# The memory norm's weights moved into the memory's weight tiles, with a TensorE warm-up on zeros (two-layer encoder, one core)

## The chip, the cores and the metric

The kernel runs on one core of a Trainium2 chip. A core has a matrix engine (TensorE, PE in the profile; its weight loads are shown apart as PEld), a vector engine (VectorE, DVE), an activation engine (ScalarE, ACT), a general one (GpSimd, POOL) and a sequencer that only issues transfers (SyncE, SP). Each engine works through its own instructions in order and waits on semaphores for the others. The metric is the device time of one execution in microseconds (us), less is better.

## The reference

Two layers over 512 tokens of 1024 features. In each layer the tokens and the 256 rows of a memory are normalised, the normalised memory is projected to keys and values, tokens attend to it, and the result joins another mixer's. What matters here is the memory's part:

```
def rmsnorm(x, g):
    xf = x.astype(jnp.float32)
    y = xf * lax.rsqrt(jnp.mean(xf * xf, axis=-1, keepdims=True) + EPS)
    return (y * g.astype(jnp.float32)).astype(x.dtype)
...
    kv = jnp.einsum('bnd,de->bne', mem_h, w_kv).reshape(Bn, N, 2, MEM_HEADS, HEAD_DIM)
    k = rmsnorm(kv[:, :, 0], kn_g)
    v = kv[:, :, 1]
...
    for i in range(DEPTH):
        h = rmsnorm(x, norm_g[i])
        mem_h = rmsnorm(mem, mem_norm_g[i])
...
        o_mem = memory_attention(q_mem, mem_h, w_mem_kv[i], mem_qn_g[i], mem_kn_g[i])
```

`mem` and its rows' factors are the same in both layers; only the norm's weights `mem_norm_g[i]` (1024 per layer) differ.

## The kernel before

**Products.** Matmuls run in a 32-bit format of fewer mantissa bits (`F32R`). Each factor is split into a high part, rounded, and a low part, the rest: a product is high x high and high x low (`mm_early`, L176 and L177) and, once the weights' low part is there, low x high (`mm_late`, L180). Weights come from `wall`, tiles of 128 x 1024 (512 KB), in the order of `PLAN`/`SEQ`. For each tile `W.hi` casts the high part on ACT (L323, `wl` to `wh`) and `W.lo` subtracts on DVE (L333, `wo`); `wh` and `wo` have four buffers each (`RING`). The first eight tiles, kind "T2", are the memory's key and value weights of layer 0; eight of kind "T2b" are those of layer 1. Two tiles feed the two pieces of a group of eight early and four late matmuls.

**Activations.** A block of tokens or memory is normalised (squares on ACT, L523, or L1132 for the memory; the sum, `mse`, and the power, `rstd`, on POOL, L483 and L484; the multiply by factor and row of weights on DVE, `norm_2`, L530), transposed in 128 x 128 pieces on PE against an identity (`turn4`, L536), and split by `split` (high on ACT, L164, or on DVE, L166; low on DVE, L167) into `act` tiles for the memory, or kept as f32 for x.

**The head** (from L1048). The identity comes by a DMA of ACT's queue (L1054). SP's queue first brings `row0`, the 1024 memory weights of layer 0 as one row (4 KB, L1056), then halves and tiles of the memory `m`, weight tiles two by two, x's row of weights and four tiles of x. `spread` (L1118) multiplies a column of ones by `row0`, so that PSUM holds the weights on all partitions; `times` (L1128) multiplies the memory by them on DVE; `turn4` and `split` make the `act` blocks, named (b, j): rows b*128 and up, features j*512 and up. The rows' factors aren't applied there: `square` and `factor` (L1132 to L1140) put them into `rm`, by which `ev_k` scales the squares of the keys (`head_sq`, L629) and the keys' factor (L694), and `ev_v` the values (L707). `ahead` is called from inside the first projection, and makes (1, 0) and the next weight tiles in the first group, and (0, 1), (1, 1) in the second.

**Layer 1.** `mem_norm(1)` loads the memory again and layer 1's weights as a row on all partitions (`row_load`), multiplies by `rm` and the row (`norm_2`, four DVE operations), transposes and splits; `ev_k` and `ev_v` then need no factor.

**Order.** The instructions of each engine stand in the order in which the code is run: the head is written out, and after it a `Driver` calls generators slot by slot. Nothing reorders them later; a transfer of SP waits for the eighth before it.

Of the kernel before, what the change touches and what calls it, by code (L numbers as in the profile page):

```python
# [10 lines left out]
F32 = mybir.dt.float32  # L11
F32R = mybir.dt.float32r
AF = mybir.ActivationFunctionType
ALU = mybir.AluOpType
# [12 lines left out]
MEM_D = 4  # L27
PAUSE = 2
DIRECT, DIRECT_B = (7,), (3, 4, 5, 6, 7)
LO_K, TURN_K, HI_V, LO_V = (4, 4), (8, 6), (1, 6), (9, 2)  # L30
PD = 2
EO = 2, 2, 1, 2, 2, 1
YB = {"m": (2, 2), "k": (1, 1, 1), 0: (1, 2, 1), 1: (1, 2, 1)}
Y = [3, 2, 2, 2, 3, 2, 2, 1, 1, 1]
# [3 lines left out]
PLAN = ["W2"] + ["T2"] * 2 + ["W1", "W2s"] + ["W2" if c.isdigit() else "W1" for c in A_ORDER[1:]] + ["W2"] + ["O1"] * 2 + ["T2b"] * 2 + ["W1bs", "W2c"] + ["W1b"] * 4 + ["W2b", "W1o"]  # L38
# [93 lines left out]
def trunk_kernel(ctx: ExitStack, tc: tile.TileContext, x, mem, wall, norm_g, mem_norm_g, gcol,  # L132
                 qn_a, kn_a, qn_b, kn_b, ident_d, mask_d, tab_a, tab_b, out):
    nc = tc.nc
# [21 lines left out]
    def at(name="at"):  # L156
        return psum.tile([128, 512], F32, tag="at", name=name, bufs=4)
# [4 lines left out]
    def split(hi, lo, src, act=True):  # L162
        if act:
            A.copy(hi, src)  # L164
        else:
            V.tensor_copy(hi, src)  # L166
        V.tensor_tensor(lo, src, hi.bitcast(F32), ALU.subtract)  # L167
# [28 lines left out]
    class Weights:  # L196
# [80 lines left out]
        def sum(self, force=False, want=None):  # L277
# [33 lines left out]
                return True  # L311
            return False

        def hi(self, force=False):
            i = self.n_hi
            if i >= len(self.items) or not self.ripe(self.at, self.items[i], force, 1 if self.items[i][1] == "T1" and self.items[i][0] < T1_DMA else None):
                return False
            if i >= RING and self.last[i - RING] > self.g - (not force and self.items[i - RING][1] != "P"):
                return False
            self.n_hi += 1  # L320
            wh = pool.tile([128, 1024], F32R, tag="wh", name="wh", bufs=RING)
            wo = pool.tile([128, 1024], F32R, tag="wo", name="wo", bufs=RING)
            A.copy(wh, self.tile[self.items[i]])  # L323
            self.hi_at.append(self.g)
            self.op.append((wh, wo))
            return True

        def lo(self):
            i = self.n_lo
            self.n_lo += 1  # L330
            wh, wo = self.op[i]
            key = self.items[i]
            V.tensor_tensor(wo, self.tile[key], wh.bitcast(F32), ALU.subtract)  # L333
            self.lo_at[key] = self.g
            self.use(key)

# [150 lines left out]

    ident = pool.tile([128, 128], F32, name="ident")
    gc = pool.tile([128, 10], F32, name="gc")
    gk = pool.tile([128, 3], F32, name="gk")  # L490
    tabs = pool.tile([128, 2048], F32, tag="tabs", name="tabs", bufs=1)
    mask = tabs[:, 0:512]
    ropeA = tabs[:, 512:2048].rearrange("p (c b s e) -> p c b s e", c=2, b=4, s=6)
    half = pool.tile([128, 8], F32, name="half")
    rm = pool.tile([128, 6], F32, name="rm")
    ones = tabs[0:1, 0:128]
    V.memset(half, -0.5)
    V.memset(ones, 1.0)
    A.activation(small.tile([128, 1], F32, tag="sm1", name="warm"), half[:, 0:1], AF.Exp)

    class Act:
# [26 lines left out]
    def norm_2(xb, r, row, js=(0, 1)):  # L528
        for j in js:
            V.scalar_tensor_tensor(xb[j], xb[j], r, row[j], ALU.mult, ALU.mult)  # L530

    def turn4(src, hi, lo, mid=None):

        p = at("xT")
        for k in range(4):
            T.transpose(p[:, k * 128:(k + 1) * 128], src[:, k * 128:(k + 1) * 128], ident)  # L536
        p = p.rearrange("p (k t) -> p k t", k=4)
        if mid:
            mid()
        if hi is not None:  # L540
            split(hi, lo, p)
        return p
# [82 lines left out]
    def head_sq(p, n=4, by=QS):  # L625
        ss = sm(n, "hss")
        for j in range(n):
            jk = small.tile([128, 128], F32, tag="junk", name="junk", bufs=2)
            A.activation(jk, p[:, j * 128:(j + 1) * 128], AF.Square, scale=by, accum_out=ss[:, j:j + 1])  # L629
        return rstd_of(ss, n)  # L630
# [20 lines left out]
    def row_load(name, src):  # L651

        t = m4(name="row")
        nc.sync.dma_start(t, src.to_broadcast([128, D]))
        rows[name] = halves(t)
# [1 line left out]
    Ms = {}  # L657

    def mem_norm(layer):
        row_load("m", mem_norm_g[layer:layer + 1, :])  # L660
        t = [m4(name="m") for _ in range(2)]
        for b in range(2):
            nc.sync.dma_start(t[b], mem[b * 128:(b + 1) * 128])
        t = [halves(v) for v in t]
        yield MEM_D
        norm_2(t[0], rm[:, 0:1], rows["m"])
        yield 1
        norm_2(t[1], rm[:, 1:2], rows["m"])
        M = Act(NM)
        for b in range(2):  # L670
            for j in range(2):
                norm_3(t[b], M, b * 128, j)
            yield 1
        Ms[layer] = M
# [9 lines left out]
    def mem_kv(layer, M, mid=None):  # L684
        kt_ = [m4(F32R, "kmT").rearrange("p (h t) -> p h t", h=4) for _ in range(2)]
        vt_ = [m4(F32R, "vm").rearrange("p (b e) -> p b e", b=2) for _ in range(2)]
        raw = None if layer else m4(name="vr")

        def ev_k(b, p):
            r = head_sq(p) if layer else head_sq(p, by=rm[:, 2 + b:3 + b])  # L690

            def rest():
                if not layer:
                    G.tensor_scalar(r, r, rm[:, b:b + 1], None, ALU.mult)  # L694
                xn = head_mul(p, r)
                yield TURN_K[layer]
                q = transpose4(xn)
                cs = slice(b * 128, (b + 1) * 128)
                yield from put_norm(q, gk_m[layer], kt_[0][:, :, cs], kt_[1][:, :, cs], LO_K[layer])

            drv.release(rest(), 2)
            yield 1

        def ev_v(b, p):

            t = s2(name="vr") if layer else raw[:, b * 512:b * 512 + 512]
            A.activation(t, p, AF.Copy, scale=0.5 if layer else rm[:, 4 + b:5 + b])  # L707
            yield HI_V[layer]
            A.copy(vt_[0][:, b], t)
            yield LO_V[layer]  # L710
            V.tensor_tensor(vt_[1][:, b], t, vt_[0][:, b].bitcast(F32), ALU.subtract)
            yield 1

        proj_t(M, NAT[:2], ev_k, mid)
        proj_t(M, NAT[:2], ev_v)
        return kt_, vt_

# [333 lines left out]
    xt = [m4(name="x") for _ in range(4)]  # L1051
    rows = {}
    mt = [m4(name="m") for _ in range(2)]
    nc.scalar.dma_start(ident, ident_d)  # L1054
    row0 = m4(name="row0")[0:1, :]
    nc.sync.dma_start(row0, mem_norm_g[0:1, :])  # L1056
    nc.sync.dma_start(mt[0][:, 0:512], mem[0:128, 0:512])
    W.dma(2)
    nc.sync.dma_start(mt[1], mem[128:256])
# [49 lines left out]
                            grA[:, None].to_broadcast([128, 4, 6, 32]), ALU.mult)  # L1109
            yield 1  # L1110

    row = [at("row") for _ in range(2)]

    def spread(j, *cols):

        for c in cols:
            cs = slice(256 * c, 256 * c + 256)
            T.matmul(row[j][:, cs], ones, row0[:, 512 * j + 256 * c:512 * j + 256 * c + 256], start=True, stop=True, skip_group_check=True)  # L1118

    spread(0, 0, 1)  # L1120
    mb, M = [halves(t) for t in mt], Act(NM)
    ss = [sm(2, "ss") for _ in range(2)]
    mg = {}

    def times(b, j):

        t = mg[b, j] = s2(name="mg")
        V.tensor_tensor(t, mb[b][j], row[j], ALU.mult)  # L1128

    def square(b, j):  # L1130

        A.activation(s2(name="sq"), mb[b][j], AF.Square, scale=1.0 / 32.0, accum_out=ss[b][:, j:j + 1])  # L1132

    def factor(b):

        e = sm(1, "mse")
        G.tensor_tensor(e, ss[b][:, 0:1], ss[b][:, 1:2], ALU.add)
        r = rstd_of(e, 1)
        for k, by in enumerate((1.0, QS, 0.5)):
            G.tensor_scalar(rm[:, 2 * k + b:2 * k + b + 1], r, by, None, ALU.mult)  # L1140

    def place_m(b, j, act=True, p=None):

        cs = slice(b * 128, (b + 1) * 128)
        split(M.block(0, j, cs), M.block(1, j, cs), p or turn4(mg[b, j], None, None), act)

    square(0, 0)
    times(0, 0)
    spread(1, 0)
    p = turn4(mg[0, 0], None, None)  # L1150
    spread(1, 1)
    W.hi(True)
    place_m(0, 0, False, p)
    W.hi(True)
    W.lo()
    times(1, 0)
    W.lo()
    for b, j in ((1, 0), (0, 1), (1, 1)):
        square(b, j)
    for b in range(2):  # L1160
        times(b, 1)
        factor(b)

    def ahead(u, b):

        if (u, b) == (0, 0):
            place_m(1, 0)
            W.hi(True)
            W.hi(True)
        if (u, b) == (0, 1):  # L1170
            place_m(0, 1)
            place_m(1, 1)

    drv.spawn(prep(), PD)
    drv.spawn(setup(), SET_AT)
# [611 lines left out]
```

## Time and profile before

| | us |
|---|---|
| three runs | 942.2, 943.04 (median), 943.81 |
| the profiled execution's own time | 942.24 |
| its span in the profile | 940.5 |
| DVE busy | 798.6 |
| ACT busy | 691.3 |
| POOL busy | 346.0 |

The span runs from the first instruction in the profile to the last; the time has about 2 us around it. A row of the timeline has the start, the duration, the engine, the line of the code, the operation, output and input, the shapes and types, and in brackets how long the engine had been idle and what ended that. Rows with "x2" and more join neighbours, and their duration reaches from the first's start to the last's end. Operations on one engine overlap a little at their ends, so that the distance of two starts says more than a duration. A row of the windows has, for each engine, busy time and in brackets the number of operations, and at its end PE's granted clock, the DMA engines' share and GB/s.

### The profile page before, as it was taken

The numbers are of one execution on the slowest core, as the hardware profiler recorded it, in microseconds if no ns is written. First come the engines' busy times: TensorE is split into PE (matmuls) and PEld (weight loads), VectorE is DVE, ScalarE is ACT, GpSimd is POOL, SyncE is SP. The second block draws the span as 40 slices with busy tenths as digits, with TensorE's granted clock in tenths as the row PEclk, the third lists the DMA queues.
The fourth block names the chain that finished last, engine by engine and source line by source line (L and its number), as shares of the span: only waits on it lengthen the run. The fifth ranks groups of instructions, "written<-read, shape, count | busy, mean of one in ns | idle before, by whom it ended". The sixth has DMA issues, their size and how long they took to land.

```text
span 940.5 us, 16300 instructions
## 1 busy us (share of the span) xinstructions
PE 932.8 (99%) x5500; PEld 819.9 (87%) x5500; DVE 798.6 (85%) x1442; ACT 691.3 (74%) x1720; POOL 346.0 (37%) x494
## 2 busy tenths in 40 slices
PE   8999999999999999999999999999999999999998
PEld 6889888888888888888889998888988999999886
DVE  6898676879888888889788899977998998689977
ACT  7775788677768686867675667637878887789774
POOL 3411425455554545463836111114262440111123
PEclk9999999999999999999999999999999999999999
DMA  9999937869787878696867889979985686785777
GB/s 355 386 259 336 299 91 190 278 139 256 158 250 147 260 154 268 158 268 136 249 165 206 246 200 243 305 229 326 270 203 122 166 239 168 199 221 126 190 173 179
DMA packets 89429, 207.15 MB, mean 220 GB/s; under 512 B 25217, under 2 KB 34689, under 8 KB 89346
## 3 DMA queue, kind: packets, MB, share of 16 engines
q1 hardware_dynamic: 68818, 140.64, 43.4%
q0 software_dynamic: 19520, 63.97, 36.9%
q10 hardware_dynamic: 1008, 1.51, 0.4%
q8 instruction: 43, 0.70, 0.3%
q14 instruction: 40, 0.33, 0.1%
HBM read 158.31 MB, written 11.08 MB: 180 GB/s over the span
## 4 chain that ended last, share of the span: by engine, by line
PE 91%; DVE 4%; DMA 3%; ACT 1%; issue 0%; SPq 0%; DVEq 0%; ACTq 0%
PE pj L176 24%; PE pj L177 24%; PE pj L180 23%; PE qT L641 2%; DMA og<-od 2%; PE ptb L1616 1%; PE sa L1302 1%; PE oo L1410 1%; PE pt L1389 1%; DMA wl<-in_wall_dram 1%; PE xT L536 1%; PE sa L1298 1%; DVE wo L333 1%; PE ob L180 1%; PE ob L177 1%; PE ob L176 1%
## 5 line engine op out<-in xcount | busy, mean ns | idle before, releaser
L333 DVE TENSOR_TENSOR wo<-wl,wh 128x1024 fp32r<-128x1024 f32 x258 | 316.4, 1232 | 7.0 <-ACT wh L323 6.8
L323 ACT CAST wh<-wl 128x1024 fp32r<-128x1024 f32 x258 | 271.7, 1060 | 29.7 <-PE pj L177 15.6
L176 PE MATMUL pj<-wh,hS 128*128 128x512 f32 (+1 forms) x416 | 154.3, 380 | 0.0
L177 PE MATMUL pj<-wh,hS 128*128 128x512 f32 (+1 forms) x416 | 148.9, 367 | 0.0
L176 PE MATMUL pj<-wh,h 128*128 128x512 f32 (+1 forms) x312 | 115.2, 378 | 0.0
L177 PE MATMUL pj<-wh,h 128*128 128x512 f32 (+1 forms) x312 | 111.7, 367 | 0.0
L484 POOL TENSOR_TENSOR rstd<-mse,half 128x4 f32<-128x4 f32 (+2 forms) x98 | 103.0, 1051 | 8.2
L180 PE MATMUL pj<-wo,hS 128*128 128x512 f32 (+1 forms) x416 | 99.5, 366 | 0.0
L177 PEld LDWEIGHTS pj<-wh,hS 128*128 128x128 f32 x416 | 78.7, 189 | 11.3
L176 PEld LDWEIGHTS pj<-wh,hS 128*128 128x128 f32 x416 | 78.6, 189 | 11.1 <-DVE sn L420 0.2
L483 POOL TENSOR_SCALAR mse<-hss 128x4 f32<-128x4 f32 (+1 forms) x88 | 46.1, 524 | 103.2 <-ACT junk L629 95.5
L180 PEld LDWEIGHTS pj<-wo,hS 128*128 128x128 f32 x416 | 72.4, 189 | 13.1
L629 ACT ACTIVATE junk<-sn 128x128 f32<-128x128 f32 x264 | 79.3, 311 | 2.2 <-DVE sn L411 2.1
L1246 POOL TENSOR_TENSOR ta<-sn,tabs 128x128 f32<-128x128 f32 (+1 forms) x64 | 35.9, 567 | 120.1 <-DVE sn L634 92.8
L398 ACT COPY sn<-pj 128x512 f32<-128x512 f32 x122 | 67.2, 590 | 16.6 <-PE pj L180 15.8
L180 PE MATMUL pj<-wo,h 128*128 128x512 f32 (+1 forms) x312 | 74.5, 365 | 0.0
L307 POOL DMA_DIRECT2D wl<-wl x34 | 30.2, 898 | 114.8 <-DVE wo L333 74.6
L261 POOL DMA_DIRECT2D wl<-in_wall_dram x40 | 38.1, 968 | 81.6 <-DMA wl<-in_wall_dram 35.3
L420 DVE TENSOR_TENSOR sn<-pj,sn 128x512 f32<-128x512 f32 x89 | 60.8, 684 | 7.1 <-PE pj L180 6.6
L177 PEld LDWEIGHTS pj<-wh,h 128*128 128x128 f32 x312 | 59.0, 189 | 8.4
L176 PEld LDWEIGHTS pj<-wh,h 128*128 128x128 f32 x312 | 59.0, 189 | 8.2
L180 PEld LDWEIGHTS pj<-wo,h 128*128 128x128 f32 x312 | 54.3, 189 | 9.7
(283 smaller groups left out, 2366.7 us busy)
## 6 DMA issues: line engine op xcount, KB each, us to landing
wl<-in_wall_dram SPq DMA_DIRECT2D x224, 512.0 KB, 7.5
wl<-wl POOLq DMA_DIRECT2D x68, 512.0 KB, 5.5
wl<-in_wall_dram POOLq DMA_DIRECT2D x44, 512.0 KB, 8.3
od<-o SPq DMA_DIRECT2D x11, 256.0 KB, 5.1
og<-od SPq DMA_DIRECT2D x10, 256.0 KB, 9.8
x<-in_x_dram SPq DMA_DIRECT2D x4, 512.0 KB, 9.0
v0d<-sn SPq DMA_DIRECT2D x8, 256.0 KB, 10.5
acc<-in_x_dram POOLq DMA_DIRECT2D x8, 256.0 KB, 7.1
```

What stands on the lines that cost most here:

```text
L176: T.matmul(o, a, b, start=start, stop=False, skip_group_check=True)
L177: T.matmul(o, c, d, start=False, stop=False, skip_group_check=True)
L180: T.matmul(o, a, b, start=False, stop=stop, skip_group_check=True)
L261: queue.dma_start(t, wall[d], **how)
L323: A.copy(wh, self.tile[self.items[i]])
L333: V.tensor_tensor(wo, self.tile[key], wh.bitcast(F32), ALU.subtract)
L398: A.copy(t, b)
L420: V.tensor_tensor(t, b, t, ALU.subtract if q == "12" else ALU.add)
L483: G.tensor_scalar(e, ss, EPS, None, ALU.add)
L484: G.tensor_tensor(r, e, half[:, 0:n], ALU.pow)
L629: A.activation(jk, p[:, j * 128:(j + 1) * 128], AF.Square, scale=by, accum_out=ss[:, j:j + 1])
L1246: G.tensor_tensor(ta[:, 0:n], xn[:, 0:n, 0:32], ropeA[:, 0, b, s0:s0 + n], ALU.mult)
```

## The change

The memory is transposed raw in both layers. Since (m * g) W is m (g W), the norm's weights go to the weight tiles: they are loaded as 16 rows of 128 (`gm`, both layers), transposed by PE and copied to `gmc`, where column 8 * layer + k holds the weights of features 128 k to 128 k + 127 on the partitions. Of each "T2" and "T2b" tile `hi` makes two ACT activations with a column of `gmc` as scale, and `lo` two DVE multiply-and-subtract operations. `row0`, `spread`, `times` and layer 1's row with its `norm_2` go. Layer 1's keys and values take the rows' factors as layer 0's do. The identity is made on POOL from a cleared tile. PE multiplies zeros six times ahead of the first transpose and five times behind the first memory block's. The squares and factors move behind the last memory blocks.

```diff
+WARM = 6, 5
...
+        def gains(self, key):
+
+            if PLAN[key[0]] not in ("T2", "T2b"):
+                return None
+            n = 8 * (PLAN[key[0]] == "T2b") + 2 * key[2]
+            return [(slice(512 * h, 512 * h + 512), gmc[:, n + h:n + h + 1]) for h in range(2)]
...
-            A.copy(wh, self.tile[self.items[i]])
+            key = self.items[i]
+            if self.gains(key):
+                for c, g in self.gains(key):
+                    A.activation(wh[:, c], self.tile[key][:, c], AF.Copy, scale=g)
+            else:
+                A.copy(wh, self.tile[key])
...
-            V.tensor_tensor(wo, self.tile[key], wh.bitcast(F32), ALU.subtract)
+            if self.gains(key):
+                for c, g in self.gains(key):
+                    V.scalar_tensor_tensor(wo[:, c], self.tile[key][:, c], g, wh[:, c].bitcast(F32), ALU.mult, ALU.subtract)
+            else:
+                V.tensor_tensor(wo, self.tile[key], wh.bitcast(F32), ALU.subtract)
...
-    ones = tabs[0:1, 0:128]
+    zero = tabs[:, 0:128]
+    G.memset(zero, 0.0)
     V.memset(half, -0.5)
-    V.memset(ones, 1.0)
...
-        row_load("m", mem_norm_g[layer:layer + 1, :])
...
-        yield MEM_D
-        norm_2(t[0], rm[:, 0:1], rows["m"])
-        yield 1
-        norm_2(t[1], rm[:, 1:2], rows["m"])
+        yield MEM_D + 1
...
-            r = head_sq(p) if layer else head_sq(p, by=rm[:, 2 + b:3 + b])
+            r = head_sq(p, by=rm[:, 2 + b:3 + b])
...
-                if not layer:
-                    G.tensor_scalar(r, r, rm[:, b:b + 1], None, ALU.mult)
+                G.tensor_scalar(r, r, rm[:, b:b + 1], None, ALU.mult)
...
-            A.activation(t, p, AF.Copy, scale=0.5 if layer else rm[:, 4 + b:5 + b])
+            A.activation(t, p, AF.Copy, scale=rm[:, 4 + b:5 + b])
...
-    nc.scalar.dma_start(ident, ident_d)
-    row0 = m4(name="row0")[0:1, :]
-    nc.sync.dma_start(row0, mem_norm_g[0:1, :])
+    gm = s2(name="gm")[0:16, 0:128]
+    nc.scalar.dma_start(gm, mem_norm_g.rearrange("l (k p) -> (l k) p", p=128))
+    G.affine_select(ident, zero, [[-1, 128]], ALU.not_equal, 1.0, base=0, channel_multiplier=1)
...
-    square(0, 0)
-    times(0, 0)
-    spread(1, 0)
-    p = turn4(mg[0, 0], None, None)
-    spread(1, 1)
+    warm(WARM[0])
+    T.transpose(gt, gm, ident[0:16, 0:16])
+    V.tensor_copy(gmc, gt)
+    place_m(0, 0, False)
+    warm(WARM[1])
     W.hi(True)
-    place_m(0, 0, False, p)
     W.hi(True)
     W.lo()
-    times(1, 0)
     W.lo()
-    for b, j in ((1, 0), (0, 1), (1, 1)):
-        square(b, j)
-    for b in range(2):
-        times(b, 1)
-        factor(b)
...
             place_m(0, 1)
             place_m(1, 1)
+            square(0, 0)
+            square(0, 1)
+            factor(0)
+            square(1, 0)
+            square(1, 1)
+            factor(1)
```

`warm(n)` is n times `T.matmul(idle[:, 0:128], zero, zero, ...)` in f32, which nothing reads. `place_m` now transposes `mb[b][j]`, the raw memory.

Two places show how instructions move: the program's start on POOL and PE, and the memory's second halves on ACT and DVE. In the rows a line number stands first, and what an instruction waits for last; `tabs` holds the zeros (before: the ones).

POOL at the program's start, before; the ISA instruction reloads POOL's library, and the branch ends the part ahead of the program:

```order
L1783 UNCONDITIONAL_BRANCH [waits barrier_Pool_Activation_PE_DVE_SP_gather]
L1137 ISA
L1137 TENSOR_TENSOR mse<-ss 128x1 [waits Activation_49]
L483 TENSOR_SCALAR mse<-mse 128x1 [waits Pool_49]
L484 TENSOR_TENSOR rstd<-mse,half 128x1 [waits DVE_49,Pool_49]
```

and after the change:

```order
L1787 UNCONDITIONAL_BRANCH [waits barrier_Pool_Activation_PE_DVE_SP_gather]
L515 MEMSET tabs 128x128
L1069 ISA
L1069 AFFINE_SELECT ident<-tabs 128x128 [waits Pool_49]
L1135 TENSOR_TENSOR mse<-ss 128x1 [waits Activation_49]
L500 TENSOR_SCALAR mse<-mse 128x1 [waits Pool_49]
```

The reload moved from ahead of the first `mse` to ahead of the identity.

PE after the change, at its start; `gt` takes the transposed gains, `pj` the first projection, and the wait for Pool_49 at `gt` is that for the identity:

```order
L1150 MATMUL idle<-tabs 128x128 [waits Pool_49]
L1150 MATMUL idle<-tabs 128x128 x5
L1153 MATMUL gt<-ident,gm 128x16 [waits DMAHW2_49,Pool_49]
L554 MATMUL xT<-ident,m 128x128 [waits DMAHW0_49]
L554 MATMUL xT<-ident,m 128x128 x3
L1150 MATMUL idle<-tabs 128x128 x5
L177 MATMUL pj<-wh,act 128x512 [waits DVE_49,Activation_49]
```

Before, three `spread` matmuls stood first, then the four transposes of the weighted memory `mg`, one more `spread`, and the same projection.

ACT from the first weight tile on, before:

```order
L1132 ACTIVATE sq,ss<-m 128x512
L323 CAST wh<-wl 128x1024 x2
L1132 ACTIVATE sq,ss<-m 128x512 x3
L164 CAST act<-xT 128x4x128
L323 CAST wh<-wl 128x1024 x2
L164 CAST act<-xT 128x4x128 x2
L323 CAST wh<-wl 128x1024 x2
L523 ACTIVATE sq,ss<-x 128x512 x4
```

and after:

```order
L334 ACTIVATE wh<-wl,gmc 128x512 x4
L165 CAST act<-xT 128x4x128
L334 ACTIVATE wh<-wl,gmc 128x512 x4
L165 CAST act<-xT 128x4x128 x2
L1130 ACTIVATE sq,ss<-m 128x512 x4
L334 ACTIVATE wh<-wl,gmc 128x512 x4
L541 ACTIVATE sq,ss<-x 128x512 x4
```

The memory's four squares went from ahead of and between the first weight tiles and casts to between the last memory casts and the weight tiles five and six, ahead of x's squares.

DVE after the change, where the memory's second halves are split; the first two rows belong to weight tile four, the third to the low half of block (0, 1), the fourth to that of (1, 1):

```order
L348 SCALAR_TENSOR_TENSOR wo<-wl,gmc,wh 128x512 [waits DMAHW7_49,Activation_49]
L348 SCALAR_TENSOR_TENSOR wo<-wl,gmc,wh 128x512 [waits Activation_49]
L168 TENSOR_TENSOR act<-xT,act 128x4x128 [waits DMAHW0_49,DMAHW5_49,PE_49,Activation_49]
L168 TENSOR_TENSOR act<-xT,act 128x4x128 [waits PE_49]
L348 SCALAR_TENSOR_TENSOR wo<-wl,gmc,wh 128x512 [waits DVE_49,DMAHW1_49,PE_49,Activation_49]
```

The low half of (0, 1) now also waits for the two loads, the transposes and the squares of the memory's first tile: its buffer lies where that tile lay in SBUF. Before it waited only for ACT's cast and DVE itself.

More of the change, by code (lines that the diff above doesn't have):

```diff
@@ L489, in trunk_kernel @@
     gc = pool.tile([128, 10], F32, name="gc")
+    gmc = pool.tile([128, 16], F32, name="gmc")
     gk = pool.tile([128, 3], F32, name="gk")
@@ L1110, in setup @@
             yield 1
[L1112 to L1120, printed above, removed]
     mb, M = [halves(t) for t in mt], Act(NM)
     ss = [sm(2, "ss") for _ in range(2)]
[L1123 to L1128, printed above, removed]
     def square(b, j):
@@ L1140, in factor, with place_m, warm @@
             G.tensor_scalar(rm[:, 2 * k + b:2 * k + b + 1], r, by, None, ALU.mult)
-    def place_m(b, j, act=True, p=None):
-        cs = slice(b * 128, (b + 1) * 128)
-        split(M.block(0, j, cs), M.block(1, j, cs), p or turn4(mg[b, j], None, None), act)
-    square(0, 0)
-    times(0, 0)
-    spread(1, 0)
-    p = turn4(mg[0, 0], None, None)
-    spread(1, 1)
+    def place_m(b, j, act=True):
+        p = turn4(mb[b][j], None, None)
+        split(*[M.block(n, j, slice(b * 128, (b + 1) * 128)) for n in range(2)], p, act)
+    idle, gt = at("idle"), at("gt")[:, 0:16]
+    def warm(n):
+        for _ in range(n):
+            T.matmul(idle[:, 0:128], zero, zero, start=True, stop=True, skip_group_check=True)
+    warm(WARM[0])
[3 more added lines that the diff above has]
+    warm(WARM[1])
     W.hi(True)
-    place_m(0, 0, False, p)
     W.hi(True)
     W.lo()
-    times(1, 0)
     W.lo()
-    for b, j in ((1, 0), (0, 1), (1, 1)):
-        square(b, j)
-    for b in range(2):
-        times(b, 1)
-        factor(b)
     def ahead(u, b):
```

## The prediction

> **What bounds the kernel now.** I read the page's first rows, then the table of windows, then the timeline of the first 30 us.
>
> ```profile
> span 940.5 us, 16300 instructions
> PE 932.8 (99%) x5500; PEld 819.9 (87%) x5500; DVE 798.6 (85%) x1442; ACT 691.3 (74%) x1720; POOL 346.0 (37%) x494
> core 0: us, PE busy (x) PEld busy (x) DVE busy (x) ACT busy (x) POOL busy (x), PEclk, DMA share, GB/s
> 0.00:12.60 12.60, 10.34 (x28) 7.26 (x29) 6.45 (x11) 6.94 (x14) 2.15 (x11) 1.00 0.83 304
> 12.60:26.00 13.40, 13.17 (x65) 10.33 (x64) 10.49 (x14) 12.11 (x28) 8.16 (x17) 1.00 1.03 412
> 26.00:500.00 474.00, 474.00 (x2557) 406.01 (x2556) 395.74 (x786) 351.73 (x998) 223.70 (x335) 1.00 0.80 219
> 700.00:940.00 240.00, 235.53 (x1590) 215.91 (x1588) 207.41 (x352) 186.60 (x407) 54.60 (x62) 1.00 0.71 176
> ```
>
> TensorE (PE) is the bound: busy 932.8 of 940.5 us, and from 26 to 500 us without a gap. Idle time lies in the head (2.26 + 0.23 us) and the tail (4.47 us), which the change doesn't touch. So a microsecond that PE wins or loses in the first 26 us stays to the end; nothing behind absorbs it. The change lives in that head, and in layer 1's memory stage. Now the head, row by row:
>
> ```profile
> 5.08 1.11 PE L536 MATMUL xT<-ident,mg 128*128 128x128 f32 x4
> 6.17 1.04 ACT L323 CAST wh<-wl 128x1024 fp32r<-128x1024 f32 x1 [1.64 <-DMA wl<-in_wall_dram]
> 6.24 0.69 DVE L166 CAST act<-xT 128x512 fp32r<-128x512 f32 x1 [1.21 <-PE xT L536]
> 7.28 0.80 PE L176 MATMUL pj<-wh,act 128*128 128x512 f32 x1
> 9.15 0.63 PE L176 MATMUL pj<-wh,act 128*128 128x512 f32 x1
> 9.58 0.63 PE L177 MATMUL pj<-wh,act 128*128 128x512 f32 x1
> 11.56 1.42 PE L180 MATMUL pj<-wo,act 128*128 128x512 f32 x4
> 13.65 0.40 PE L176 MATMUL pj<-wh,act 128*128 128x512 f32 x1
> 13.89 0.39 PE L177 MATMUL pj<-wh,act 128*128 128x512 f32 x1
> ```
>
> The first projection matmul starts at 7.28, released by the first weight tile (landed 6.17, cast by 7.21). Equal matmuls stand 0.43 us apart at 9.15 and 0.24 at 13.65, though the windows print a granted clock of 1.00: PE starts at about half rate. It speeds up near 11.9, inside the group at 11.56.
>
> **The change, term by term.** The working is against the profiled execution's own 942.24 us.
>
> *1. The identity now waits for GpSimd (POOL).* It was a DMA. Now POOL clears 128x128, passes an ISA instruction (a reload of its library) and runs the select; the gains' transpose, the raw memory transposes and every scaled weight tile wait for it. In before the same ISA stood ahead of the first `mse`, where POOL had nothing to do:
>
> ```profile
> 10.23 0.41 POOL L1137 TENSOR_TENSOR mse<-ss 128x1 f32<-128x1 f32 x1 [9.79 <-ACT sq L1132]
> 12.51 0.20 POOL L1137 TENSOR_TENSOR mse<-ss 128x1 f32<-128x1 f32 x1
> 13.76 2.47 POOL L1140 TENSOR_SCALAR rm<-rstd 128x1 f32<-128x1 f32 x3
> L1284 POOL MEMSET p<- 128x64 f32 x8 | 3.6, 453 | 0.0
> ```
>
> It leaves no row. It fitted into the 9.79 us of idle, so the reload costs R between 0 and about 9.4 us; the first `mse` is only 0.2 longer than the second. No row stands nearer to either end, so I take the middle, **R = 4.7**, and keep both ends. A 128x64 memset takes 0.45; for the clear and the select of twice the columns I take 0.6 each (0.45 to 0.9). From about 0.8 us, where the engines enter the program, the identity stands at 0.8 + 0.6 + 4.7 + 0.6 = 6.7. Then comes the gains' transpose (0.3, one of the four at 5.08), and what took 1.85 us in before: transposes from 5.08 to the cast's end at 6.93. The gain copy and two scaled half tiles run beside it on ACT in about as long. First projection matmul: 6.7 + 0.3 + 1.85 = 8.85 against 7.28, **+1.6**. With R of 0 to 3 the weights bind instead: 6.17 and two activations, 1.36 (priced below), give 7.55, +0.3. With 9.4 it is 13.55, +6.3.
>
> [...]
>
> *2. Zeros warm TensorE.* Cold, before loses about 0.2 on each of eight matmuls, some 0.5 on four transposes, 0.1 on the L180 group: 2.2 us, the most that warming can give. Nothing at all is the other end: the identity comes well after the six first matmuls on zeros, so PE pauses again. In before the speed came about 4.6 us after the steady run began at 7.28. Counted so from the identity at 6.7, it comes at 11.3; matmuls from 8.85 to 11.3 are cold, five or six of them. Gain: 2.4 x 0.2 + 0.6 = 1.1, **-1.1**.
>
> [...]
>
> *3. The squares now stand ahead of x on ScalarE (ACT).* This is the dearest edit. In before they filled waits of 4 to 11 us; now four of them follow the second pair of memory casts.
>
> ```profile
> 8.77 0.63 ACT L1132 ACTIVATE sq<-m 128x512 f32<-128x512 f32 x1 [0.25 <-DMA m<-in_mem_dram]
> 10.05 0.62 ACT L1132 ACTIVATE sq<-m 128x512 f32<-128x512 f32 x1
> 15.03 1.03 PE L536 MATMUL xT<-ident,mg 128*128 128x128 f32 x8
> 15.72 1.07 ACT L164 CAST act<-xT 128x512 fp32r<-128x512 f32 x2 [1.29 <-issue]
> 16.33 1.29 DVE L167 TENSOR_TENSOR act<-xT,act 128x512 fp32r<-128x512 f32 x2 [0.46 <-ACT act L164]
> 16.68 2.01 ACT L323 CAST wh<-wl 128x1024 fp32r<-128x1024 f32 x2
> 17.08 0.50 PE L177 MATMUL pj<-wh,act 128*128 128x512 f32 x1
> 18.58 0.64 ACT L523 ACTIVATE sq<-x 128x512 f32<-128x512 f32 x1
> 22.71 1.06 PE L536 MATMUL xT<-ident,x 128*128 128x128 f32 x8
> 825.61 0.74 ACT L1607 ACTIVATE pb<-pb,rdb 128x512 f32<-128x512 f32 x1
> 826.24 0.59 ACT L1620 CAST pbT<-ptb 128x512 fp32r<-128x512 f32 x1
> ```
>
> Squares of one block follow at 0.64 (8.77 to 10.05 is two). A 128x512 activation with a scale from a column, the form of the new `wh`, takes 0.74 and lets the next one start after 0.63: a tile 1.26 to 1.37, a pair 2.55. Count from the start of the eight transposes, at 15.03 before. Before: casts at +0.69, weights at +1.65, the first square of x at +3.55, x's transposes on PE at +7.68; PE's own work ahead of them is as long, so x is just in time. After: casts to +1.65, four squares to +4.2, the weight pair to +6.8, the first square of x there. From that square to x's transposes before took 22.71 - 18.58 = 4.13 (square, POOL's rstd, DVE's multiply, all still there), so they come at +10.93: **+3.25** later.
>
> A second wait lies inside it and adds nothing: the low half of (0,1) on DVE now waits for both squares of block 0 (the order in the section on the change). It starts at 1.65 + 1.28 = +2.93 instead of +1.30, so PE's second matmul of that group, at +2.05 before, slips by some 1.6; the other 1.65 is lost at x. Behind the waiting instruction on DVE stand the other low half and the next two weight tiles' lows. The slower weight pair in front, 0.65 more, goes into ACT's 1.29 idle before 15.72; were that gone, it would cost 0.65. POOL's two factor chains now run ahead of x's rstd. The first took 2.3 us (10.23 to 12.51), the second 3.7 (to 16.23, its three small products 2.47); from +2.93, two of the short kind end at +7.5, one of each at +8.9, and x's two squares end near +8.1. So they cost nothing or up to 0.8; I take nothing, since the first is the plain case.
>
> *4. Layer 1.* Each pair of the memory's weight tiles costs ACT 0.6 more, k's eight squares take the memory's factor as a scale, and DVE's lows become two multiply-and-subtract halves; four DVE multiplies by the row go.
>
> ```profile
> L333 DVE TENSOR_TENSOR wo<-wl,wh 128x1024 fp32r<-128x1024 f32 x258 | 316.4, 1232 | 7.0 <-ACT wh L323 6.8
> L530 DVE SCALAR_TENSOR_TENSOR m<-m,rm,row 128x512 f32<-128x512 f32 x4 | 2.8, 746 | 0.0
> L629 ACT ACTIVATE junk<-pj,rm x8: 353/372/386, 21.0 to 28.4; 128x128 f32<-128x128 f32 x8
> L629 ACT ACTIVATE junk<-pj x8: 263/294/317, 644.1 to 647.8; 128x128 f32<-128x128 f32 x8
> 640.00:650.00 10.00, 10.00 (x50) 8.38 (x49) 7.19 (x10) 9.43 (x30) 5.19 (x8) 1.00 1.04 355
> 650.00:660.00 10.00, 10.00 (x62) 8.88 (x61) 9.81 (x13) 4.51 (x8) 4.77 (x5) 1.00 1.04 247
> 660.00:670.00 10.00, 10.00 (x85) 9.81 (x84) 10.00 (x14) 9.81 (x23) 0.00 (x0) 1.00 0.98 198
> ```
>
> ACT gains 4 x 0.6 + 8 x 0.08 = 3.0 us over the stage and has 0.57 free in 640 to 650; DVE gains 8 x (1.49 - 1.23) = 2.1, saves 2.8 earlier, and is full from 650 to 670. PE has never waited here. Between nothing (the buffers carry it) and some 1.6 (what ACT's 3.0 leaves after 640 to 650's 0.57 and half as much again beside it) I take **+0.8**. That eight weight tiles in layer 0 cost DVE the same lies in its 2.9 us of idle from 12.6 to 26.
>
> *5. At nothing:* the rank-1 matmuls and DVE products of the old head lie ahead of 7.28 or beside cold matmuls; two loads less on SP bring the rest 0.4 us earlier, and ACT and DMA hide that; POOL's extra multiply in layer 1 has half an idle engine around it.
>
> **Sum:** 1.6 - 1.1 + 3.25 + 0.8 = +4.55, 946.8. The profiled run sits at the low end of the three (942.2 to 943.81, median 943.04); I add 0.4, half its distance: **947.2 us**.
>
> **Rivals.**
>
> *A short reload* (R up to 3): 0.3 - 2.2 + 3.25 + 0.8 = +2.15, 944.8 with the 0.4; without layer 1's term 944.0. For it: `mse` was only 0.2 longer. Against: 9.79 us of idle could hide any size.
>
> *A long reload* (R near 9.4): 6.3 - 1.1 + 3.25 + 0.8 = +9.25, 951.9. Some of it would go where late PE work finds all weights ready.
>
> *It delivers, and ends faster.* One mechanism: warm PE from the first matmul brings the second transposes so early that x's landing, not ACT, releases x.
>
> ```profile
> 8.76 0.98 SPq L1068 DMA_DIRECT2D x<-in_x_dram  x2
> x<-in_x_dram SPq DMA_DIRECT2D x4, 512.0 KB, 9.0
> ```
>
> Issued at 8.76, landing after about 9.0: x is there at 17.8, or 17.4 with the earlier queue. x's transposes then come at 17.4 + 4.13 = 21.5 against 22.71: -1.2, about 941.0 and with the 0.4 up to 941.4. ACT would have to reach x's square at 17.4, so the second transposes would have to start at 10.6; warm and with a free reload they start at 15.03 + 0.3 - 2.2 = 13.1. It decides in its favour only if ACT's squares and weights cost less than half of the rows above.
>
> *It doesn't do what it says:* the zeros don't warm PE. That takes the 1.1 away: 948.3.
>
> **How the numbers follow.** A measurement of this kernel can tell about 0.2%, 1.9 us, from no change. Forecast (R from 3 to 8, warm or not): 0.52. Short reload 0.25, of which 0.15 is within 0.2% and 0.10 above. Long reload 0.13. Delivered 0.10, 0.07 of it faster. So faster 0.07, same 0.18, slower 0.75. The range 942.5 to 951.0 leaves out the delivered case and the upper part of the long reload.
>
> **What would show it.** In the new profile: the select's row on POOL near 6.1 and POOL idle ahead of it (term 1); matmul spacing in the first group of eight, 0.43 or 0.23 (term 2); x's first square on ACT about 6.8 us behind the eight transposes, with PE waiting at L178 of the second block and at x's transposes (term 3); PE below 10.00 in a window between 640 and 670 (term 4). The select at 2 us, or a square of x before 18.6, would prove me wrong.

## The result

| | us | runs |
|---|---|---|
| before | 942.62 (941.09 to 943.81) | 6 |
| after the change | 948.52 (947.80 to 949.47) | 6 |

The ratio is 1.0065, with a 95% interval from 1.0054 to 1.0076: the change costs 5.9 us. The profiled execution took 948.40 us by itself, 6.16 more than the one before. In the experiments further down four executions took over 1020 us (one each of e6 and e12, two of the kernel before); the ratios leave them out.

The page of the changed kernel, and its windows (columns as before), with one window of the kernel before at the end:

```profile
span 946.6 us, 16353 instructions
PE 932.9 (99%) x5515; PEld 821.6 (87%) x5515; DVE 796.6 (84%) x1450; ACT 697.0 (74%) x1736; POOL 355.5 (38%) x498
...
0.00:12.60 12.60, 10.62 (x48) 8.70 (x49) 5.96 (x11) 6.41 (x10) 0.69 (x6) 1.00 0.87 307
12.60:26.00 13.40, 9.19 (x47) 7.11 (x46) 7.97 (x14) 12.39 (x35) 7.86 (x19) 1.00 1.03 410
26.00:40.00 14.00, 14.00 (x67) 11.62 (x65) 13.16 (x19) 12.39 (x30) 6.23 (x12) 0.88 1.03 410
640.00:660.00 20.00, 19.30 (x98) 15.99 (x97) 12.84 (x21) 16.58 (x43) 9.40 (x14) 1.00 1.05 332
660.00:700.00 40.00, 38.17 (x256) 34.99 (x255) 38.32 (x52) 31.91 (x77) 16.87 (x17) 1.00 0.94 242
...
660.00:700.00 40.00, 40.00 (x256) 36.05 (x255) 37.80 (x51) 33.10 (x87) 15.85 (x16) 1.00 1.02 261
```

PE's busy time is the same as before to 0.1 us; the span is 6.1 longer, so the loss shows as idle PE: 4.2 us from 12.6 to 26 (0.23 before), 0.7 from 640 to 660 and 1.83 from 660 to 700 (none before). PE also runs slowly for a stretch: the granted clock of 0.88 over 14 us is 3.4 us at half rate. That lies inside the busy time, and is offset there, by the head's faster start among others. The timeline names the places.

The head's timeline after the change, the rows that answer to those of before:

```profile
0.72 0.20 POOL L515 MEMSET tabs<- 128x128 f32 x1 [0.29 <-POOLq L1780]
1.00 0.29 POOL L1069 TENSOR_SCALAR_AFFINE_SELECT ident<-tabs 128x128 f32<-128x128 f32 x1
4.99 1.33 ACT L334 ACTIVATE wh<-wl,gmc 128x512 fp32r<-128x512 f32 x2 [2.77 <-DMA wl<-in_wall_dram]
6.56 0.48 PE L177 MATMUL pj<-wh,act 128*128 128x512 f32 x1
6.88 0.39 PE L178 MATMUL pj<-wh,act 128*128 128x512 f32 x1
7.11 0.40 PE L177 MATMUL pj<-wh,act 128*128 128x512 f32 x1
...
13.40 1.04 PE L554 MATMUL xT<-ident,m 128*128 128x128 f32 x8
16.86 1.29 DVE L168 TENSOR_TENSOR act<-xT,act 128x512 fp32r<-128x512 f32 x2 [2.42 <-ACT sq L1130]
16.91 0.19 POOL L1135 TENSOR_TENSOR mse<-ss 128x1 f32<-128x1 f32 x1 [15.61 <-ACT sq L1130]
17.60 0.50 PE L178 MATMUL pj<-wh,act 128*128 128x512 f32 x1 [1.94 <-DVE act L168]
19.47 0.68 POOL L1135 TENSOR_TENSOR mse<-ss 128x1 f32<-128x1 f32 x1
20.40 0.62 ACT L541 ACTIVATE sq<-x 128x512 f32<-128x512 f32 x1
21.96 0.79 POOL L1138 TENSOR_SCALAR rm<-rstd 128x1 f32<-128x1 f32 x3
22.70 0.19 POOL L543 TENSOR_TENSOR mse<-ss 128x1 f32<-128x1 f32 x1
25.36 1.09 PE L554 MATMUL xT<-ident,x 128*128 128x128 f32 x8 [2.27 <-DVE x L548]
...
27.29 0.63 PE L178 MATMUL pj<-wh,act 128*128 128x512 f32 x1
27.71 0.63 PE L177 MATMUL pj<-wh,act 128*128 128x512 f32 x1
29.42 1.37 PE L181 MATMUL pj<-wo,act 128*128 128x512 f32 x4
```

Read it by comparing equal instructions. The identity is there at 1.29, the first projection matmul starts at 6.56 instead of 7.28, and its neighbours stand 0.23 apart: PE is at full rate by 6.88, and the second transposes come at 13.40 instead of 15.03, **1.63 early**. Then DVE waits for the squares of block 0 (16.86), PE for DVE (1.94 at 17.60), and x's transposes come at 25.36 instead of 22.71, **2.65 late**. From 26.5 on matmuls stand 0.42 apart, and the late group at 29.42 is 3.96 behind. The later rows, first of before, then of after:

```profile
25.46 1.07 PE L180 MATMUL pj<-wo,act 128*128 128x512 f32 x4
646.96 1.03 PE L536 MATMUL xT<-ident,acc 128*128 128x128 f32 x8
649.10 0.69 DVE L634 TENSOR_TENSOR xn<-pj,rstd 128x512 f32<-128x512 f32 x1 [1.26 <-POOL rstd L484]
663.34 2.01 ACT L323 CAST wh<-wl 128x1024 fp32r<-128x1024 f32 x2
666.08 0.39 PE L176 MATMUL pj<-wh,hS 128*128 128x256 f32 x1
```

```profile
642.60 2.55 ACT L334 ACTIVATE wh<-wl,gmc 128x512 fp32r<-128x512 f32 x4
651.06 1.06 PE L554 MATMUL xT<-ident,acc 128*128 128x128 f32 x8 [0.70 <-DVE acc L548]
654.47 0.69 DVE L652 TENSOR_TENSOR xn<-pj,rstd 128x512 f32<-128x512 f32 x1 [1.67 <-POOL rstd L707]
669.39 2.00 ACT L336 CAST wh<-wl 128x1024 fp32r<-128x1024 f32 x2
672.13 0.38 PE L177 MATMUL pj<-wh,hS 128*128 128x256 f32 x1 [1.82 <-DVE sn L437]
```

At 651.06 PE is 4.10 late, at 672.13 6.05, and so it stays to the end. In between DVE's `xn`, the keys times their factors, waits for POOL's extra multiply by `rm` (L707) and is 5.37 late.

### The profile page after: what moved, and what is told of

Read it like the earlier page. It is cut to its first block, busy times and chain, and to the rows that moved or that the text cites. A ratio compares the mean times of both kernels' runs of the same rounds, so it can differ in the third digit from the quotient of the medians.

```text
span 946.6 us, 16353 instructions
## 1 busy us (share of the span) xinstructions
PE 932.9 (99%) x5515; PEld 821.6 (87%) x5515; DVE 796.6 (84%) x1450; ACT 697.0 (74%) x1736; POOL 355.5 (38%) x498
## 4 chain that ended last, share of the span: by engine, by line
PE 91%; DVE 4%; ACT 2%; DMA 1%; POOL 1%; issue 1%; SPq 0%; DVEq 0%; ACTq 0%; POOLq 0%
PE pj L177 24%; PE pj L178 24%; PE pj L181 23%; PE qT L659 3%; PE sa L1306 2%; PE oo L1414 2%; PE pt L1393 1%; PE ptb L1620 1%; PE sa L1302 1%; DVE wo L350 1%; PE xT L554 1%; PE ob L181 1%; PE ob L178 1%; PE ob L177 1%; PE sb L172 1%; PE sb L171 1%
## 5 line engine op out<-in xcount | busy, mean ns | idle before, releaser
L350 DVE TENSOR_TENSOR wo<-wl,wh 128x1024 fp32r<-128x1024 f32 x242 | 295.6, 1225 | 7.2 <-ACT wh L336 7.1
L336 ACT CAST wh<-wl 128x1024 fp32r<-128x1024 f32 x242 | 255.9, 1062 | 22.8 <-PE pj L178 15.1
```

Source lines behind the costliest of these rows:

```text
L336: A.copy(wh, self.tile[key])
```

## The experiments

Each ran beside the kernel before, whose median lay between 941.48 and 942.66 in these comparisons. So a difference of two medians from different comparisons can be off by up to a microsecond, and the ratios are the safer measure. Theory: three separate costs, the squares' new place in the head, layer 1's slower weight tiles and factors, and PE's half rate behind a long wait. The kernels are called e1 to e12 here.

**e1, the squares early.** The changed kernel, with this edit:

```diff
+    square(0, 0)
     W.hi(True)
     W.hi(True)
+    square(1, 0)
+    square(0, 1)
     W.lo()
     W.lo()
+    factor(0)
...
             W.hi(True)
             W.hi(True)
+            square(1, 1)
+            factor(1)
...
-            square(0, 0)
-            square(0, 1)
-            factor(0)
-            square(1, 0)
-            square(1, 1)
-            factor(1)
```

> The changed kernel with the memory's four squares and the factors back in ACT's early gaps: (0,0) ahead of the first weight tile, (1,0) and (0,1) behind the second, (1,1) behind the fourth. Theory (the squares' new place costs the head): DVE's low half of (0,1) waits only for its cast, so the 1.94 us of PE idle at 17.6 go; x's first square on ACT comes near 18.0 instead of 20.40, x's transposes near 22.1 instead of 25.36, PE waits about 1 us there instead of 2.27, and no half-rate stretch follows. Against before, PE stands at -0.6 us behind 40 us instead of +4.16; time about 943.8. Rival (the two activations for each weight tile hold x, and the squares only fill ACT's gaps): x's transposes stay at 24 or later, time about 947.

Measured: 944.45 us, ratio 1.0023 (1.0013 to 1.0033), 4.1 less than the change. From its timeline:

```profile
17.20 0.63 ACT L541 ACTIVATE sq<-x 128x512 f32<-128x512 f32 x1
21.27 1.09 PE L554 MATMUL xT<-ident,x 128*128 128x128 f32 x8 [0.80 <-DVE x L548]
```

x's transposes come 1.44 before those of the kernel before, the wait at 17.6 is gone. The same slower weight tiles as in the change stand ahead of x here, so they alone don't hold it to 24; the rival falls. The head has no half rate (granted clock 1.00 from 12.6 to 40), but layer 1 has a stretch of it, where PE again waited 1.82 (at 666.64) for DVE:

```profile
660.00:680.00 20.00, 18.18 (x140) 17.94 (x139) 17.30 (x22) 17.63 (x36) 4.24 (x5) 0.91 1.00 270
```

In the change the same wait was followed by full rate (1.00 from 660 to 700).

**e2, layer 1 as before.**

```diff
-            if PLAN[key[0]] not in ("T2", "T2b"):
+            if PLAN[key[0]] != "T2":
...
+        row_load("m", mem_norm_g[layer:layer + 1, :])
...
-        yield MEM_D + 1
+        yield MEM_D
+        norm_2(t[0], rm[:, 0:1], rows["m"])
+        yield 1
+        norm_2(t[1], rm[:, 1:2], rows["m"])
...
-            r = head_sq(p, by=rm[:, 2 + b:3 + b])
+            r = head_sq(p) if layer else head_sq(p, by=rm[:, 2 + b:3 + b])
```

and likewise for `r` times `rm` and the scale in `ev_v`.

> The changed kernel with layer 1's memory as before (row of weights, four DVE multiplies, plain weight casts, no factor in keys and values). Theory (ACT's and DVE's extra work in layer 1 makes the two waits of PE at 651.06, 0.70, and at 672.12, 1.83): both go, the shift against before stays at about +3.3 from 580 us to the end, time about 945.7. Rival (they are the late head's, passed on): 948.5 as it is.

Measured: 945.08, ratio 1.0027 (1.0017 to 1.0037), 3.4 less than the change. Its windows:

```profile
12.60:20.00 7.40, 5.46 (x22) 4.07 (x21) 4.43 (x7) 6.42 (x16) 3.26 (x8) 0.82 1.03 414
660.00:680.00 20.00, 20.00 (x166) 19.84 (x166) 18.50 (x24) 18.93 (x41) 5.29 (x6) 1.00 1.02 273
```

PE doesn't wait in layer 1 any more, though the head, which is the same code as in the change, is late here too: x's transposes come at 24.69, 1.98 behind those of before (2.65 in the change). So layer 1's waits are its own and not the head's passed on. The 0.82 in the first row was not expected: the half rate now lies between 17 and 21, behind the other wait of the head.

**e3, the second factor late.**

```diff
             square(1, 1)
-            factor(1)
...
                 n[c] = norm_1(xb[c], c == 2)
+                if c == 0:
+                    factor(1)
```

> The changed kernel with the second memory factor on POOL moved behind x's first rstd. Theory (the second factor chain held x's mse from 21.73 to 22.70): x's transposes come 1.0 earlier, at 24.4, PE waits 1.3 there instead of 2.27. Time 947.5 if a wait of 1.3 still halves the rate afterwards, 946.0 if it doesn't. Rival (x is held by ACT's squares of x alone): 948.5, x's transposes at 25.3.

Measured: 947.03, ratio 1.0055 (1.0042 to 1.0067): 1.5 less in the median, 0.9 by the ratio, and the intervals overlap. POOL now takes x's `mse` as soon as ACT's second square of x is done:

```profile
21.57 0.19 POOL L543 TENSOR_TENSOR mse<-ss 128x1 f32<-128x1 f32 x1 [2.29 <-ACT sq L541]
24.30 1.05 PE L554 MATMUL xT<-ident,x 128*128 128x128 f32 x8
```

In the change that `mse` stood behind `rm` at 22.70, so the second factor chain held x by about a microsecond. Behind that, PE came to x's transposes without a wait: half rate behind the 1.94 us wait (0.82 from 12.6 to 20, 0.93 from 20 to 26) had made PE itself late.

**e4, PE busy ahead of x.**

```diff
+            if c == 2:
+                idle2 = at("idle")
+                for _ in range(8):
+                    T.matmul(idle2[:, 0:128], ident, ident, start=True, stop=True, skip_group_check=True)
             if 1 < c < 4:
                 first_t(H, xb[c - 2], c - 2)
```

> The changed kernel with eight f32 matmuls of the identity by itself, which nothing reads, on PE ahead of x's first transposes, where PE waited 2.27 us. Theory (the wait halves PE's rate for the 3.4 us from 26.4, and that costs 1.5): granted clock 1.00 instead of 0.88 from 26 to 40 us, matmul spacing 0.23 throughout, time 947.0. Rival (the rate falls for another reason, such as the load of all engines at that time): 0.88 again and 948.5 or more.

Measured: 948.92, ratio 1.0067 (1.0054 to 1.0081): no gain. The granted clock was 1.00 from 26 to 40, but the half rate had moved ahead, behind the wait of 1.94 at 16.8, as in e2 (0.87 from 12.6 to 26), and another stretch followed the wait of 1.82 in layer 1 (0.91 from 660 to 680). So the experiment didn't tell what it was for, and e9 was made.

**e5, e1 and e2 together.**

> Both edits together: squares early as in e1, layer 1 as before as in e2. Theory (the head's and layer 1's losses are separate and add): PE stands at -1.4 us against before from x's transposes on, as in e1, some 0.7 more is won where before waited near 540 and 577, and PE doesn't wait in 640 to 700; time about 940.3, below before. Rival (something later in layer 1 waits for the clock of the loads, so that an earlier head is given back): 942.3, as before.

Measured: 941.01, ratio 0.9990 (0.9981 to 0.9999): slightly below before, and 7.5 under the change, which is the sum of e1's 4.1 and e2's 3.4. Its timeline and windows:

```profile
21.58 1.09 PE L554 MATMUL xT<-ident,x 128*128 128x128 f32 x8 [1.01 <-DVE x L548]
640.00:660.00 20.00, 20.00 (x116) 17.52 (x115) 18.10 (x25) 13.97 (x35) 9.95 (x12) 1.00 1.04 303
660.00:680.00 20.00, 20.00 (x156) 19.28 (x155) 18.50 (x25) 17.16 (x40) 3.99 (x4) 1.00 1.04 293
```

The two losses are separate. What is left of the change (raw transposes, gains in layer 0's weights, identity from POOL, zeros) is worth about a microsecond, only just outside the interval.

**e6, e5 without the zeros** (`WARM = 0, 0`).

> e5 without the eleven matmuls on zeros. Theory (the zeros bring full rate at about 6 us instead of 12, and the head is now short enough for it to count): the first group's matmuls stand 0.43 apart until about 10, the second transposes start 1 to 1.5 later, and x's with them; time 941.3 to 941.8. Rival (x's transposes come at a time that ACT's work sets by itself): 940.3 as in e5.

Measured: 941.81, ratio 0.9995 (0.9985 to 1.0004). The intervals of e5 and e6 overlap; the timeline shows the mechanism:

```profile
7.08 0.63 PE L177 MATMUL pj<-wh,act 128*128 128x512 f32 x1
7.50 0.63 PE L178 MATMUL pj<-wh,act 128*128 128x512 f32 x1
...
22.39 1.07 PE L554 MATMUL xT<-ident,x 128*128 128x128 f32 x8 [0.68 <-issue]
```

Without zeros the matmuls stand 0.42 apart, with them 0.26 at 6.70 (e5), and x's transposes come 0.81 later than in e5, as much as the medians differ.

**e7 and e8, the two halves of layer 1's change**, both on e1. In e7 the tiles take the gains, and the memory is multiplied by its factor on DVE:

```diff
-        yield MEM_D + 1
+        yield MEM_D
+        for b in range(2):
+            for v in t[b]:
+                V.tensor_scalar(v, v, rm[:, b:b + 1], None, ALU.mult)
+            if not b:
+                yield 1
```

with keys and values as in e2. In e8 the memory is multiplied by the row of weights, the tiles are cast plainly, and keys and values take the factor:

```diff
-        yield MEM_D + 1
+        yield MEM_D
+        for b in range(2):
+            for j in range(2):
+                V.tensor_tensor(t[b][j], t[b][j], rows["m"][j], ALU.mult)
+            if not b:
+                yield 1
```

> e1 with only the weights' part in layer 1: its tiles scaled by the gains, the memory multiplied by its factor on DVE (four tensor_scalar), keys and values without a factor. Theory (two activations and two multiply-and-subtracts for each tile cost layer 1's waits): 943.5 to 944.5, the wait of 1.8 near 666 stays. Rival (the factor on the keys' squares and POOL's product cost them): about 941.

> e1 with only the factor's part in layer 1: the memory multiplied by the row of weights on DVE (four tensor_tensor), plain weight casts, the factor in keys and values. Theory of e7: about 940.5 to 941.2, no wait near 666, at most some 0.5 at x's transposes near 645. Rival: 943.5 to 944.5.

Measured: e7 943.12, ratio 1.0013 (1.0005 to 1.0022); e8 941.90, ratio 0.9997 (0.9988 to 1.0006). Against e5 the gains cost 2.1 and the factor 0.9; e1, with both, 3.4. The windows of e7, then of e8:

```profile
660.00:680.00 20.00, 18.91 (x152) 18.40 (x152) 18.60 (x24) 18.94 (x41) 4.09 (x5) 1.00 1.01 278
```

```profile
660.00:680.00 20.00, 19.32 (x161) 19.09 (x160) 18.47 (x24) 19.00 (x41) 5.33 (x6) 1.00 0.99 268
```

PE waits 1.09 with the gains alone, 0.68 with the factor alone and 1.82 with both: neither rival holds whole, the gains weigh more. The earlier wait of 0.70, at the transposes of layer 1's tokens, goes with the gains: PE is busy 19.29 of the 20 us from 640 to 660 in e7 and all of them in e8. With it the two halves make 1.8 and 0.7 of waiting, in sum the 2.5 of both. The factor's part runs over POOL: in e8 DVE's `xn` waits 1.67 for the product with `rm` as in the change, in e7 1.25 for `rstd`, as before. (e8's profiled execution was its slowest run, 943.89, with a wait of 1.08 near 582 that no other profile has; only its medians are compared.)

**e9, both waits of the head filled**: e4's edit, and nine such matmuls behind `place_m(1, 1)` in `ahead`.

> The changed kernel with f32 matmuls of the identity by itself in both waits of PE in the head: nine behind the eight second transposes (the 1.94 us before 17.6), eight ahead of x's transposes as in e4. [...] Rival (the half rate comes from the load, or costs nothing because x's chain holds PE anyway): 948.5.

Measured: 948.26 (946.16 to 949.83), ratio 1.0068 (1.0055 to 1.0081). Its profiled execution, the fastest of its runs, has no half rate in the head:

```profile
12.60:20.00 7.40, 7.40 (x46) 6.30 (x45) 4.43 (x8) 6.42 (x16) 3.40 (x8) 1.00 1.03 413
20.00:26.00 6.00, 5.51 (x38) 4.87 (x37) 3.55 (x7) 6.00 (x21) 5.18 (x13) 1.00 1.03 408
26.00:40.00 14.00, 14.00 (x75) 11.84 (x74) 13.18 (x19) 12.33 (x28) 5.49 (x11) 1.00 1.03 410
```

With the long waits of the head filled its half rate is gone in this profile; that it costs 1.5 in the median does not show.

**e10, two squares early**: block 0's squares and factor as in e1, block 1's as in the change.

> The changed kernel with only block 0's two squares and its factor early, block 1's left between the last casts and the weight tiles. Theory (two costs of the new place, ACT's time ahead of x and the low half's wait for block 0's squares): the wait of 1.94 goes whole; x's first square on ACT comes 1.3 earlier, near 19.1, and POOL no longer holds x, so x's transposes come near 23.0, +0.3 against before; time between 944.8 (no half rate) and 946.3 (half rate behind PE's longer wait at x). Rival (what is late at x is the weight pair, not the squares): 24.5 or later, 947.5.

Measured: 945.98, ratio 1.0049 (1.0037 to 1.0062).

```profile
18.36 0.62 ACT L541 ACTIVATE sq<-x 128x512 f32<-128x512 f32 x1
22.44 0.77 PE L554 MATMUL xT<-ident,x 128*128 128x128 f32 x5 [1.82 <-DVE x L548]
```

Half of the squares gives back 2.9 of x's lateness, where e1 gives back 4.1, and the low half's wait of 1.94 goes. In the time it gives 2.5 of e1's 4.1 by the medians, but 1.5 of 4.0 by the ratios. The wait of 1.82 at x's transposes was followed by full rate (1.00 from 20 to 40), one of 1.81 in layer 1 by half rate (0.91 from 660 to 680).

**e11, the move alone, on the kernel before**: its squares and factors where the change has them.

> The kernel before with nothing but the squares and factors moved to where the change has them (no gains in the weights, no zeros, identity by DMA). Theory (this move alone is what delays x): ACT does 2.6 us more between the second casts and x's first square, POOL's second factor holds x by up to 1, x's transposes come 2.6 to 3.6 later, at 25.3 to 26.3; time 944.7 to 945.7, up to 1.7 more where a stretch of half rate follows. Rival (only the squares together with slower weight tiles are too much): 943 or less.

Measured: 945.95, ratio 1.0048 (1.0034 to 1.0061): the move alone costs 4.5 of 941.48.

```profile
21.26 0.63 ACT L523 ACTIVATE sq<-x 128x512 f32<-128x512 f32 x1
26.77 1.63 PE L536 MATMUL xT<-ident,x 128*128 128x128 f32 x8 [2.19 <-issue]
```

x's transposes are 4.06 late with plain weight casts ahead of them. No slower weight tile is needed, and the rival falls. (The profiled execution was the slowest of this kernel's runs, 948.17; behind x's late transposes it has a granted clock of 0.88 from 26 to 40.)

**e12, e2 with both waits filled as in e9.**

> e2 (layer 1 as before) with both waits of the head filled as in e9, so that PE has no wait over a microsecond left before 700 us; beside e2 it shows the price of the half rate in the medians. Theory (a half-rate stretch in nearly every run of e2, at 1.0 to 1.5 each): no granted clock under 1.00 before 700 us, PE near +1.9 against before at x's transposes, time 943.7 to 944.1 against e2's 945.08. Rival (the half rate mostly falls where x's chain holds PE anyway, so that it costs nothing in the median): 945.1.

Measured: 944.67, ratio 1.0025 (1.0014 to 1.0036), against e2's 945.08 and 1.0027. The profile has no half rate up to 700 us (granted clock 1.0 over the whole execution, 1.00 from 12.6 to 40 and from 640 to 700), and x's transposes come at 24.77, +2.06 against before. A gain of 0.4 with such intervals decides nothing between the theory's 1.0 to 1.4 and nothing.

## Why the prediction was right, and which steps were not

The forecast of 947.2, slower, in 942.5 to 951.0, is met by 948.52. Its sum of +4.55 stands against +6.16 between the two profiled executions, and the terms came out differently. Of its own signs x's first square, the two waits of the head, the spacing and layer 1's windows bear it out. An early select on POOL (at 2 us) it had named as what would prove it wrong, and the select came at 1.00.

1. **The identity's wait, +1.6: wrong.** The step that failed is the middle value of R, 4.7. POOL's select starts 0.08 after its clear ends; the ISA instruction between them, called a reload in the prediction, costs no more than that. That it reloads anything, and what a reload would take, no row shows. The first matmul came 0.72 earlier than before: the rival's short reload, whose own +0.3 was too high because the first weight tile landed at 4.99 instead of 6.17.
2. **The zeros, -1.1: right in mechanism and near in size.** Full rate from 6.9 on (0.23 between equal matmuls); with the earlier start the second transposes came 1.63 early, 0.91 of it beyond the start; PE lost 0.76 at 8.51 to a wait for the second weight tile. e6 puts the zeros' share in a repaired head at 0.8, by intervals that overlap.
3. **The squares on ACT, +3.25: right in place, a term short.** Counted from the second transposes, x's first square was forecast at +6.8 and came at +7.00 (13.40 to 20.40). PE's wait for the low half was forecast at 1.6 and was 1.94. But x's transposes came at +11.96, not +10.93: the second factor chain on POOL held x's `mse` to 22.70. The prediction had bounded that at 0.8 and taken nothing; e3 shows about a microsecond at x's `mse`. In all the move from -1.63 to +2.65 is 4.28. e1 and e11, the two ways of moving the squares alone, give 4.1 and 4.5 in the medians. That the low half's wait adds nothing of its own wasn't tried by itself; e10 removes it together with two squares.
4. **Layer 1, +0.8: too small, and its upper bound of 1.6 too.** PE waited 0.70 and 1.82, and e2 gives back 3.4. The bound took what ACT couldn't absorb in one place; the delay passed from ACT's scaled casts (642.60) and POOL's extra multiply to DVE's `xn` (654.47, 5.37 late), through DVE's lows back to ACT's next casts (669.39, 6.05 behind those of before at 663.34, when PE was some 4.1 behind), and nothing between absorbed it. POOL's multiply stood at nothing in the prediction, because POOL was half idle; but an engine waited for its result (1.67 at `xn` instead of 1.26). The waits are 2.5 in sum. That the rest of the 3.4 is half rate behind the second of them, which e1, e4 and e10 have in their profiles and the change, e3 and e9 don't, fits but isn't shown.
5. **Not foreseen: PE's half rate behind its own waits.** It is seen in the profile (0.88 from 26 to 40; x's transposes +2.65, the late group behind them +3.96). Its price in the medians stays open: e9 and e12 took it out of their profiled executions, and their medians are 0.3 to 0.7 under those of the change, e4 and e2, while the ratios are the same within 0.0003: too little to tell it from nothing. A hint lies in the granted clock of each run as a whole: within each kernel, over the 97 runs of the change and of e1 to e12 that took under 951 us, a run with 0.001 less was on average 0.4 us longer. One stretch (1.7 us lost in some 945) is 0.0018, so by this estimate it costs some 0.7 us, less than the 1.3 seen in the profile.

So that the time fell near the forecast is in good part luck: a term that was 2.3 too dear for POOL's reload hid three that were too cheap: POOL's factor (1.0), layer 1 (2.6 by the medians, POOL's multiply and any half rate there included) and, in the profiled execution, the head's half rate (1.3). Not all of these are lost whole at the end: before waited 0.27 near 539, and between 40 and 580 us PE won back 0.5 to 0.9 of its lateness, here and in e2.

## What to carry to other kernels

Small work that sits in an engine's early waits is free there and dear where the next stage's input waits behind it in the same queue: the memory's four squares, 2.6 us of ACT, cost 4 us once they stood ahead of x. When a factor is moved from activations into weights, price the weights' stage by the chain through all engines that feed it, not by one engine's free time in one window. A faster start is worth only what the next bound lets through: here the head began 0.7 us earlier, ran at full rate from 6.9 us (0.23 between matmuls) and was 1.6 ahead, and all of it was lost at the next wait.

## What the runs showed of the hardware

- The ISA instruction ahead of POOL's select left no gap to speak of: 0.08 us between the clear's end at 0.92 and the select's start at 1.00 (the change).
- PE fell to half rate (0.43 between equal matmuls instead of 0.23) for a stretch of about 3.4 us behind a wait of some 2 us, though it had worked right up to the wait. Granted clocks of 0.88 over 14 us (the change), and of 0.82 over 7.4 with 0.94 over the next 6 us (e2), both come to 3.4 us. A wait of about a microsecond didn't do it (e5, 1.01 at 21.58, granted clock 1.00 from 20 to 40). The length alone didn't decide: a wait of 1.94 at 17.60 was followed by full rate in the change's profile (1.00 from 12.6 to 26), and the same wait at 16.94 in e2 by half rate; the wait of 1.8 in layer 1 was followed by half rate in e1, e4 and e10 (0.91 from 660 to 680), and by full rate in the change, e3 and e9 (1.00). What else decides, these runs don't show.
- With eleven matmuls on zeros ahead of it the first group had 0.23 between matmuls at 6.88 (the change); without them it had 0.42 at 7.08 (e6).
